# Attention of a two-layer diffusion step: eight of the gates' modulation blocks on VectorE from a ring of their own, two units a round on TensorE, output tiles in the last round

## The chip, the cores and the metric

The kernel runs on one core of a Trainium2 chip. The time is that of one execution on the device in microseconds; a kernel's time is the median of several executions. Beside it stands one execution taken with the hardware profiler, whose trace gives start and length of every instruction.

The names used below: TensorE (PE in the profile) multiplies matrices and turns 128x128 blocks, ScalarE (ACT) and VectorE (DVE) work element by element, GpSimd (POOL) does little here, SyncE (SP) issues nearly all transfers. PSUM is the memory of eight banks that TensorE writes; ScalarE and VectorE read it.

## The reference, cut to what matters

One step of a backbone with two layers, for 384 tokens (128 of a prompt, 256 of a sample, a grid 64 wide) and a model width of 1024, all in float32. Each layer is a mixer and a gated ConvFFN, each with an adaptive norm ahead of it and a gate on its residual. The change lies in the attention mixer of layer 0.

```python
mod = silu(cond) @ w_ada + b_ada            # (2, 6*1024): one row for the prompt, one for the sample
sm, cm, gm, sf, cf, gf = split(mod, 6)      # shift, scale, gate of the mixer; the same of the FFN
# layer 0, mixer
h = rmsnorm(x, g) * (1 + cm) + sm
q, k, v = qkv_proj(h, w_qkv)                # 16 heads of 64
# prompt tokens: softmax(q k^T / 8) v among themselves
# sample tokens: softmax over (window of the grid, with a bias per head, and 128 cached context keys)
x = x + gm * (attn(q, k, v) @ w_o)
# layer 0, FFN
h = rmsnorm(x, g2) * (1 + cf) + sf
x = x + gf * (silu(conv(h @ w_up_gate)) * conv(h @ w_up_value)) @ w_down
# layer 1 likewise, its mixer a gated MLP over chunks; then a last rmsnorm
# outputs: y of prompt and sample, and the keys and values of the prompt
```

## The kernel before, in words

**Layout and products.** Everything is kept with features on the 128 partitions and tokens along the row: `x[k]`, k = 0..7, is 128x384. A float32 product is made of three matmuls on halves: `split` (lines 116 to 118) rounds a tensor to `hi` on ScalarE and takes `lo` = source − `hi` on VectorE, and `mac` (lines 110 to 114) adds hi·hi, hi·lo and lo·hi. A tile of output (128x384 out of 8 row blocks) is thus 24 matmuls. A unit of weights (128x1024, 512 KB) comes through one of three staging buffers `st`, is split by `ready` into one of five `hi`/`lo` pairs, and is fetched three units ahead by SyncE's queue. The normalized input `h` is kept as `hhi`, `hlo` (8 blocks each).

**Modulations.** Layer 0's SM and CM are made ahead of the attention. The other pieces are made in one of two ways. `Ada` (lines 167 to 221) makes layer 0's GM, SF and CF on TensorE: a unit is one row block k of one piece, loaded (512 KB, tile `adw`) and multiplied in four small matmuls at four column positions (line 197), 24 units in all. After k = 7 ScalarE copies the sums out (`ada_sb`, line 202), and `flush`, called ahead of the next unit, turns them with two transposes (line 213) into a bank that VectorE adds the bias from (line 215; for CF also line 126). `AdaV` (lines 225 to 259) makes all the others, 56 blocks, on VectorE: two dot products of a 128x1024 block with the broadcast silu(c) (line 255, one for each of the two rows c) and an add (line 257). Those run in the FFNs and the gMLP. All blocks of both classes go through one ring of four buffers `adw`.

**Rounds.** The attention runs in eight rounds t = 0..7, one pair of heads each. The order of the instructions on TensorE, ScalarE, VectorE and SyncE is as the code is written (`tc.manual_schedule`, left at `written.__exit__`); behind that a scheduler orders them. One round, b = 0, 1 being the two blocks of 128 sample queries:

1. `scores(0)` (line 612: six pairs of matmuls, prompt queries included), then SyncE issues the next round's cached keys (`kT`) and bias rows (`btr`); `exps(0)`: on VectorE bias and maximum in one pass (line 619, into `st`), on ScalarE the exponentials with their sums (line 629).
2. `turn` of the last round's first head (lines 644, 646), `normalized` (a reciprocal, line 634, and products, line 636), ScalarE's copies of the turned blocks (`pT`, lines 651, 652).
3. `products` with the next pair's key weights (24 matmuls), `ready` for the next unit, `scores(1)`, and `keys(t+1)`: ScalarE copies two parts of the products beside the cached part in `kT` (lines 567, 568), then splits all 512 columns into `khi` and `klo`.
4. `exps(1)`, `turn` of the other head, `normalized`; `products` with the next query weights, `ready`, `bias` (line 602: the next round's bias in `bt`), `queries` (`qhi` line 577 on ScalarE, `qlo` line 578 on VectorE).
5. `values(t-1)` (line 661, split into `ohi`, `olo`), `ada.run(3)`, and the loads of three further units.

TensorE's queue, and each of the others, is worked off strictly in this order, so a wait on one engine holds what is written behind it.

**Last round.** It has no products. `ada.run(3)` stands between `scores(1)` and the turning. Then the output projection: tiles m = 0..3 start on the blocks k = 0..5, take blocks 6 and 7 as the last two rounds' values arrive; `flush` of CF; the four tiles' last blocks with `residual` (line 382: x += gate · bank, two instructions a tile, and ScalarE's squares for the next norm). Behind the written order come tiles 4 to 7 with their residuals, then the FFN (`norm_first`): on VectorE, GpSimd and ScalarE the root of the mean square (lines 317 to 321) and its spread `R` (line 359), then the last blocks of `h` (lines 334 to 338), while TensorE starts on the blocks that are ready. There `ada_v.start` loads silu's input and ScalarE makes silu(c) (line 246).

## Time and profile before

| | us |
|---|---|
| median of three runs | 1010.93 (1010.9 to 1011.51) |
| the profiled execution | 1011.21 |
| its span (first to last instruction) | 1009.4 |
| granted TensorE clock, mean | 0.997 |
| first round's first line 619 on VectorE | 68.83 |
| eighth round's | 176.10 |
| the FFN's first matmul behind the output tiles | 224.90 |

A span counts from the first instruction; the execution's time has 1.8 us more around it. All times of rows are from the span's start. A row of the timeline reads: start, length of the instruction or of the joined group, engine, line, operation, output<-input, sizes, count, and in brackets the idle time ahead of it and what ended it. A row of the windows gives for one stretch the busy time and count of TensorE, its weight loads, VectorE, ScalarE and GpSimd, then the granted clock as a share of full speed, the share of the DMA engines and GB/s. A row of the waits gives the total of a kind of wait, how often it came and the longest.

### The profile page before, as it was taken

To read this page: it belongs to the slowest core of one execution; us is meant where nothing else is said; L and a number is where in the kernel's file an instruction comes from. 1 tells how busy PE (TensorE), PEld (TensorE's weight loads), DVE (VectorE), ACT (ScalarE), POOL (GpSimd) and SP (SyncE) were. 2 spreads that over 40 slices of the span, in tenths; PEclk is the share of its full clock that TensorE was granted. 3 is DMA by queue.
4 is the path that set the end of the run, shared out by engine and by line. 5 is a ranking of instruction groups with operands and counts; after the bars stand their busy time and mean duration, and the time that the engine had idled before them with its cause. 6 is when DMAs were issued, how large, how long until landed. Compare 5 with 4: busy or idle time off the path is not lost.

```text
span 1009.4 us, 15920 instructions
## 1 busy us (share of the span) xinstructions
PE 991.1 (98%) x6007; PEld 940.8 (93%) x6008; DVE 778.3 (77%) x1597; ACT 479.8 (48%) x839; POOL 15.8 (2%) x31
## 2 busy tenths in 40 slices
PE   8999999999999999999999999999999999999996
PEld 6788888799999999999998889999999999999996
DVE  5656666488999888999889999687598777777652
ACT  4455655467655454433463334433385444443331
POOL 1000000000000000000000000000000000000000
PEclk9999999999999999999999999999999999999999
DMA  8766465634465554567728765466235434345521
GB/s 332 284 217 209 167 214 168 225 116 135 127 201 167 150 163 144 180 213 224 237 97 272 237 191 181 161 201 187 94 91 166 140 125 126 126 115 168 167 73 63
DMA packets 53020, 172.96 MB, mean 171 GB/s; under 512 B 6016, under 2 KB 11152, under 8 KB 52944
## 3 DMA queue, kind: packets, MB, share of 16 engines
q1 hardware_dynamic: 51840, 169.33, 51.8%
q0 software_dynamic: 528, 1.32, 0.3%
q10 hardware_dynamic: 576, 1.31, 0.3%
q8 instruction: 47, 0.77, 0.3%
q14 instruction: 29, 0.24, 0.1%
HBM read 169.31 MB, written 2.62 MB: 170 GB/s over the span
## 4 chain that ended last, share of the span: by engine, by line
PE 92%; DMA 3%; DVE 2%; ACT 1%; issue 1%; POOL 0%; POOLq 0%; SPq 0%; ACTq 0%
PE bank L113 28%; PE bank L114 28%; PE bank L112 28%; DMA kT<-in_ckT 1%; PE bank L883 1%; PE bank L661 1%; PE bank L644 1%; PE bank L612 1%; PE bank L150 1%; PE bank L197 1%; DMA adw<-in_w_ada 1%; DMA lo<-in_x 0%; PE bank L449 0%; POOL ry L319 0%; PE bank L291 0%
## 5 line engine op out<-in xcount | busy, mean ns | idle before, releaser
L105 ACT CAST hi<-st 128x1024 fp32r<-128x1024 f32 (+1 forms) x184 | 189.3, 1030 | 296.2 <-PE bank L113 237.6
L114 PE MATMUL bank<-hhi,lo 128*128 128x384 f32 (+1 forms) x960 | 325.0, 339 | 0.2 <-DVE lo L118 0.2
L113 PE MATMUL bank<-hlo,hi 128*128 128x384 f32 (+1 forms) x960 | 324.7, 338 | 0.0
L112 PE MATMUL bank<-hhi,hi 128*128 128x384 f32 (+1 forms) x960 | 324.6, 338 | 0.0
L106 DVE TENSOR_TENSOR lo<-st,hi 128x1024 fp32r<-128x1024 f32 (+1 forms) x184 | 220.1, 1198 | 64.6 <-ACT hi L105 64.5
L114 PEld LDWEIGHTS bank<-hhi,lo 128*128 128x128 f32 x960 | 181.1, 189 | 0.5 <-DVE lo L118 0.5
L112 PEld LDWEIGHTS bank<-hhi,hi 128*128 128x128 f32 x960 | 181.0, 189 | 0.4 <-ACT kT L568 0.2
L113 PEld LDWEIGHTS bank<-hlo,hi 128*128 128x128 f32 x960 | 180.4, 188 | 0.1
L255 DVE CUSTOM_DVE_ANT_0 junk<-adw,cs 128x1024 bf16<-128x1024 f32 x112 | 136.5, 1219 | 1.0
L113 PE MATMUL bank<-alo,hi 128*128 128x384 f32 x352 | 118.3, 336 | 0.0
L114 PE MATMUL bank<-ahi,lo 128*128 128x384 f32 x352 | 118.3, 336 | 0.0
L112 PE MATMUL bank<-ahi,hi 128*128 128x384 f32 x352 | 118.1, 336 | 0.0
L114 PEld LDWEIGHTS bank<-ahi,lo 128*128 128x128 f32 x352 | 66.2, 188 | 0.0
L113 PEld LDWEIGHTS bank<-alo,hi 128*128 128x128 f32 x352 | 66.2, 188 | 0.0
L112 PEld LDWEIGHTS bank<-ahi,hi 128*128 128x128 f32 x352 | 66.2, 188 | 0.0
L112 PE MATMUL bank<-hi,hhi 128*128 128x512 f32 x144 | 58.1, 403 | 0.4 <-ACT hhi L440 0.4
L113 PE MATMUL bank<-lo,hhi 128*128 128x512 f32 x144 | 56.9, 395 | 0.1
L114 PE MATMUL bank<-hi,hlo 128*128 128x512 f32 x144 | 56.7, 394 | 0.0
L382 DVE SCALAR_TENSOR_TENSOR x<-bank,mod,x 128x128 f32<-128x128 f32 x64 | 23.8, 412 | 34.6 <-PE bank L114 34.5
L113 PE MATMUL bank<-mlo,hi 128*128 128x384 f32 x128 | 43.6, 341 | 0.0
L112 PE MATMUL bank<-mhi,hi 128*128 128x384 f32 x128 | 43.3, 338 | 0.0
L114 PE MATMUL bank<-mhi,lo 128*128 128x384 f32 x128 | 43.3, 338 | 0.0
(174 smaller groups left out, 1279.6 us busy)
## 6 DMA issues: line engine op xcount, KB each, us to landing
st<-in_w_up SPq DMA_DIRECT2D x88, 512.0 KB, 3.6
adw<-in_w_adaT SPq DMA_DIRECT2D x56, 512.0 KB, 3.6
adw<-in_w_ada SPq DMA_DIRECT2D x40, 512.0 KB, 5.6
st<-in_w_down SPq DMA_DIRECT2D x32, 512.0 KB, 3.6
st<-in_w_qk SPq DMA_DIRECT2D x16, 512.0 KB, 3.5
st<-in_w_gu SPq DMA_DIRECT2D x16, 512.0 KB, 4.1
st<-in_w_gv SPq DMA_DIRECT2D x16, 512.0 KB, 4.3
st<-in_w_gout SPq DMA_DIRECT2D x16, 512.0 KB, 4.6
```

Of the source, the lines that this page charges most:

```text
L105: nc.scalar.copy(hi[:, :n], st[:, :n])
L106: nc.vector.tensor_tensor(lo[:, :n], st[:, :n], hi[:, :n].bitcast(F32), ALU.subtract)
L112: nc.tensor.matmul(out, a[0], b[0], start=start, stop=False)
L113: nc.tensor.matmul(out, a[0], b[1], start=False, stop=False)
L114: nc.tensor.matmul(out, a[1], b[0], start=False, stop=stop)
L150: nc.tensor.matmul(pa[32 * j:32 * j + 32, 0:P], cond_s[:, 4 * hf + kk, :], w[hf][:, kk, P * q:P * q + P], start=(kk == 0), stop=(kk == 3), ...
L197: nc.tensor.matmul(self.pa[32 * j:32 * j + 32, 0:256], cond_s[:, k, :], t[:, 256 * j:256 * j + 256], start=(k == 0), stop=(k == KD - 1), t ...
L255: tc.keep_in_program_order(nc.vector.tensor_tensor_reduce(self.junk, t, self.cs[c], 1.0, 0.0, ALU.mult, ALU.add, m[:, c:c + 1]))
L382: nc.vector.scalar_tensor_tensor(x[m][:, a:b], ps[:, a:b], mod(l, gate, m, c), x[m][:, a:b], ALU.mult, ALU.add)
L612: nc.tensor.matmul(sc[hh][:, cols], q[qp][HS[hh], qs:qs + P], k[kp][HS[hh], ks], start=i == 0, stop=i == 2)
L644: nc.tensor.transpose((ta[:, o:o + P] if g < 2 else tb[:, o - 512:o - 512 + P]), pr[:, b, g * P:g * P + P], ident)
L661: nc.tensor.matmul(pv[64 * hh:64 * hh + 64, cols], vv[:, P * t + 64 * hh:P * t + 64 * hh + 64], pT[hh][:, o:o + n], start=start, stop=stop ...
```

## The change

**Rings and shares.** The ring of four becomes two rings of two, `adw` and `adb`. `Ada` keeps SF and CF alone: 16 units, two ahead of the rounds, two in each of rounds 0 to 6, none in the last. GM of layer 0 goes to `AdaV` as eight blocks in ring `adb`. For these, silu(c) is made ahead of the first keys, and each round does one block on VectorE: one dot product (`half(0)`) behind `exps(0)`, the other with the add (`half(1)`) behind the second `normalized`. `AdaV`'s other 56 blocks stay where they were and use both rings in turn.

**Keys.** `keys` splits three parts (128 cached columns, and 256 and 128 columns straight from the products' bank) into `khi` and `klo` with no copy ahead; the prompt's keys for the output are copied by ScalarE afterwards (`sk`).

**Order within a round.** The next pair's cached keys and bias rows are issued one round earlier, ahead of the modulation loads on SyncE. `bias` moves up between `exps(1)` and `normalized`. `flush` has its own place between the second products and `values`.

**Last round.** It leaves the loop behind `exps(1)`; output tiles 0 and 1 stand between its steps, `flush` of CF comes between tile 1 and `values(6)`, tile 2 around `values(7)`. Tiles 3 to 7 are in the written order, each with the residual of the tile three before it; residuals 5 to 7 are behind it. `ohi` and `olo` of blocks 6 and 7 lie in `hhi` and `hlo`, which the products no longer need then.

```diff
-ADA_BUFS = 4
+ADA_BUFS = 2
...
-            order = [(0, GM), (0, SF), (0, CF)]
+            order = [(0, SF), (0, CF)]
...
         def one(self, l, pc, k, t):
-            self.flush()
...
+            self.todo = (one(0, GM) + both(1, SM, CM)[:8]
...
+        def half(self, c, l, pc, k, t):
+            m = mods[l][:, pc, k]
+            tc.keep_in_program_order(nc.vector.tensor_tensor_reduce(
+                self.junk, t, self.cs[c], 1.0, 0.0, ALU.mult, ALU.add, m[:, c:c + 1]))
+            if c:
                 nc.vector.tensor_scalar(m, m, b_ada[:, l, pc * 8 + k:pc * 8 + k + 1], None, ALU.add)
...
-        def keys(t, kT, p):
-            nc.scalar.copy(kT[:, 0:256], p[:, 0:256])
-            nc.scalar.copy(kT[:, 384:512], p[:, 256:384])
-            nc.gpsimd.dma_start(skT_out[:, t, :], kT[:, 0:NPR])
+        def keys(t, ck, p):
             k = [wkp.tile([P, 512], F32R, name=n, tag=n) for n in ("khi", "klo")]
-            split(*k, kT)
+            for o, src in ((256, ck), (0, p[:, 0:256]), (384, p[:, 256:384])):
+                s = slice(o, o + src.shape[1])
+                split(k[0][:, s], k[1][:, s], src)
+            sk = wkp.tile([P, NPR], F32, name="sk", tag="sk", bufs=1)
+            nc.scalar.copy(sk, p[:, 0:NPR])
+            nc.gpsimd.dma_start(skT_out[:, t, :], sk)
...
             e = exps(0, sc, pr, pc)
+            ada_v.half(0, *blocks[0])
...
+            bias(btr)
             normalized(*e)
-            if not last:
-                p = products()
-                ready()
-                bias(btr)
-                Q = queries(p)
-                if old is not None:
-                    values(t - 1, pT)
-                ada.run(3)
-                ada.load(3)
+            ada_v.half(1, *blocks.pop(0))
+            p = products()
+            ready()
+            Q = queries(p)
+            ada.flush()
+            if old is not None:
+                values(t - 1, pT)
+            if t < NPAIR - 2:
+                kT, btr = cache(t + 2), bias_load(t + 2)
+            ada.run(2)
+            ada.load(2)
+            if t < NPAIR - 2:
+                blocks.append(ada_v.load(1))
...
         output(0, range(6), ps_mm)
+        pT.append(turned(1, turn(*old[1])))
+        normalized(*e)
         ready()
-        values(6, pT, ps_sc)
+        pv = bank(ps_sc)
         output(1, range(6), ps_sc)
+        ada.flush()
+        values(6, pT, pv)
         ready()
+        ada_v.half(1, *blocks.pop(0))
...
-        output(2, range(7), ps_mm)
-        ready()
+        output(2, range(5), ps_mm)
         values(7, pT)
-        output(3, range(7), ps_sc)
-        ada.flush()
-        for m in range(4):
+        output(2, (5, 6))
+        for m in range(3):
             output(m, (7,))
-            residual(0, GM, m, out[m][1], (0, SF, CF))
-            if m == 1:
+        for m in range(3, KD):
+            output(m, range(KD), (ps_sc, ps_ta, ps_ad, ps_mm, ps_sc)[m - 3])
+            if m < KD - 1:
                 ready()
+            residual(0, GM, m - 3, out[m - 3][1], (0, SF, CF))
         written.__exit__(None, None, None)
-        for m in range(4, KD):
-            output(m, range(KD), ps_mm if m % 2 else ps_sc)
-            if m < KD - 2:
-                ready()
+        for m in range(KD - 3, KD):
             residual(0, GM, m, out[m][1], (0, SF, CF))
```

VectorE in a middle round, from the split of the keys to the split of the queries, as it stands before (line 619 with its `ISA` rows is the bias with the maximum, line 634 the reciprocal, line 602 the bias for the next round):

```order
159 L118 TENSOR_TENSOR klo<-kT,khi 128x512
160 L619 ISA bank,st<-bank,bt 128x384
161 L619 ISA st 128x1
162 L619 ISA bank,st<-bank,bt 128x384
163 L619 ISA st 128x1
164 L634 RECIPROCAL st<-st 128x2
165 L636 TENSOR_SCALAR pr<-pr,st 128x384 x2
166 L118 TENSOR_TENSOR lo<-st,hi 128x1024
167 L602 TENSOR_TENSOR bt<-mask,btr 128x3x128 x2
168 L578 SCALAR_TENSOR_TENSOR qlo<-bank,qhi 128x384
```

The same place behind the change, where line 636 is the bias with the maximum, line 619 the next round's bias, line 260 the dot product of `half` and line 263 its add:

```order
184 L118 TENSOR_TENSOR klo<-ck,khi 128x128
185 L118 TENSOR_TENSOR klo<-bank,khi 128x256
186 L118 TENSOR_TENSOR klo<-bank,khi 128x128
187 L636 ISA bank,st<-bank,bt 128x384
188 L636 ISA st 128x1
189 L636 ISA bank,st<-bank,bt 128x384
190 L636 ISA st 128x1
191 L619 TENSOR_TENSOR bt<-mask,btr 128x3x128 x2
192 L651 RECIPROCAL st<-st 128x2
193 L653 TENSOR_SCALAR pr<-pr,st 128x384 x2
194 L260 ISA junk,mod_129<-adb,cs_628 128x1024
195 L260 ISA mod_129 128x1
```

The subtraction of the keys is in three parts, the bias stands ahead of the reciprocal, and the dot product stands between the normalized rows and the weights' `lo`, which with `qlo` follows as before.

TensorE at the end of a round in which a piece of `Ada` has been completed, before (`pT`, `V` are `values`, `adw` with `cond_s` the units, `ident` with `ada_sb` the flush, `khi` with `qhi` the next scores):

```order
441 L661 MATMUL bank<-pT,V 64x256 x2
442 L661 MATMUL bank<-pT,V 64x128 x2
443 L197 MATMUL bank<-adw,cond_s 32x256 x8
444 L213 MATMUL bank<-ident,ada_sb 128x128 x2
445 L197 MATMUL bank<-adw,cond_s 32x256 x4
446 L612 MATMUL bank<-khi,qhi 128x384 x2
```

And behind the change:

```order
562 L215 MATMUL bank<-ident,ada_sb 128x128 x2
563 L678 MATMUL bank<-pT,V 64x256 x2
564 L678 MATMUL bank<-pT,cv 64x256 x2
565 L678 MATMUL bank<-pT,V 64x256 x2
566 L678 MATMUL bank<-pT,V 64x128 x2
567 L199 MATMUL bank<-adw,cond_s 32x256 x8
568 L629 MATMUL bank<-khi,qhi 128x384 x2
```

The two transposes no longer stand between two units of the same round; they stand ahead of `values`, a round behind the last unit of their piece.

VectorE where the residuals start, before (`olo` rows are `values` of pairs 6 and 7, lines 215 and 126 the bias and gain of CF, line 382 the residual):

```order
248 L118 TENSOR_TENSOR olo_169<-bank,ohi_161 128x384
249 L118 TENSOR_TENSOR lo<-st,hi 128x1024 x2
250 L118 TENSOR_TENSOR olo_170<-bank,ohi_162 128x384
251 L215 TENSOR_TENSOR mod_129<-bank,b_ada 128x16
252 L126 SCALAR_TENSOR_TENSOR mod_129<-mod_129,prm 128x16
253 L382 SCALAR_TENSOR_TENSOR x_99<-bank,mod_129,x_99 128x128
```

And behind the change (`hlo` from `bank` is now the values' rest):

```order
301 L217 TENSOR_TENSOR mod_129<-bank,b_ada 128x16
302 L126 SCALAR_TENSOR_TENSOR mod_129<-mod_129,prm 128x16
303 L118 TENSOR_TENSOR hlo<-bank,hhi 128x384
304 L118 TENSOR_TENSOR lo<-st,hi 128x1024
305 L260 ISA junk,mod_129<-adb,cs_628 128x1024
306 L260 ISA mod_129 128x1
307 L263 TENSOR_SCALAR mod_129<-mod_129,b_ada 128x2
308 L118 TENSOR_TENSOR hlo<-bank,hhi 128x384
309 L118 TENSOR_TENSOR lo<-st,hi 128x1024
310 L394 SCALAR_TENSOR_TENSOR x_99<-bank,mod_129,x_99 128x128
```

CF's bias and gain stand ahead of both values' subtractions and no longer between the last values and the first residual.

More of the change, by code (lines that the diff above doesn't have):

```diff
@@ L129, in gain, with ada_tile @@
             ALU.add, ALU.mult)
+    def ada_tile(ring):
+        tag = ("adw", "adb")[ring % 2]
+        return adp.tile([P, D], F32, name=tag, tag=tag)
     def ada_load(f, late=False):
@@ L134, in ada_load @@
         for hf in range(2):
-            st = adp.tile([P, D], F32, name="adw", tag="adw")
+            st = ada_tile(hf)
             if late:
@@ L181, in load @@
                 l, pc, k = self.todo.pop(0)
-                t = adp.tile([P, D], F32, name="adw", tag="adw")
+                t = ada_tile(0)
                 nc.sync.dma_start(t, w_ada[k * P:(k + 1) * P, (pc - GM) * D:(pc - GM + 1) * D])
@@ L259, in run @@
                     gain(l, pc, slice(k, k + 1))
+        def run(self, n):
+            for _ in range(n):
+                block = self.load(len(self.todo))
+                for c in range(2):
+                    self.half(c, *block)
     ada_v = AdaV()
@@ L407, in attention @@
         cv = pool.tile([P, D], F32, name="cv")
-        ohi = [pool.tile([P, NT], F32R, name=f"ohi{t}") for t in range(NPAIR)]
-        olo = [pool.tile([P, NT], F32R, name=f"olo{t}") for t in range(NPAIR)]
+        ohi = [pool.tile([P, NT], F32R, name=f"ohi{t}") for t in range(6)] + [hhi[:, t, :NT] for t in (6, 7)]
+        olo = [pool.tile([P, NT], F32R, name=f"olo{t}") for t in range(6)] + [hlo[:, t, :NT] for t in (6, 7)]
         acc = [bank(q) for q in (ps_mm, ps_mm, ps_mm, ps_sc, ps_sc, ps_ta)]
@@ L509, in attention @@
             sb = ada_products(aw.pop(k + 1))
+            if k == 5:
+                ada_v.start(csp)
             if k + 3 < KD:
@@ L653, in turned, with values @@
             return pT
-        def values(t, pT, pool=ps_mm):
-            pv = bank(pool)
+        def values(t, pT, pv=None):
+            pv = bank(ps_mm) if pv is None else pv
             def part(hh, cols, vv, o, n, start, stop):
@@ L676, in attention @@
         nc.sync.dma_start(cv, cv_in)
-        ada.load(3)
+        ada.load(2)
+        blocks = [ada_v.load(1) for _ in range(2)]
         ready()
@@ L683, in attention @@
         v_out(1)
+        ada_v.silu()
+        ada_v.junk = tmp.tile([P, D], BF16, name="junk", tag="R0")
         nc.gpsimd.dma_start(sv_out, V[:, 0, :])
@@ L690, in attention @@
         Q = queries(p)
+        kT, btr = cache(1), bias_load(1)
+        ada.run(2)
+        ada.load(2)
         old = None
@@ L908, in gmlp @@
             residual(1, GM, m, ps, (1, SF, CF))
+    csp = ctx.enter_context(tc.tile_pool(name="cs", bufs=1))
     with tc.tile_pool(name="att", bufs=1) as pool, tc.tile_pool(name="attw", bufs=2) as wkp:
         attention(pool, wkp)
[L913 to L914 removed]
+    ada_v.junk = csp.tile([P, D], BF16, name="junk")
     with tc.tile_pool(name="ffn0", bufs=1) as pool, tc.tile_pool(name="ffn0w", bufs=2) as wkp:
```

45 lines of the change are left out of this document (18 added, 27 removed).

## The prediction

> **What bounds the kernel now.** I read the page first, then the waits of TensorE between 60 and 226 us, then the timeline of VectorE and TensorE there. The page:
>
> ```profile
> span 1009.4 us, 15920 instructions
> PE 991.1 (98%) x6007; PEld 940.8 (93%) x6008; DVE 778.3 (77%) x1597; ACT 479.8 (48%) x839; POOL 15.8 (2%) x31
> ```
>
> TensorE is busy 98% of the span, so a gain must come out of work taken from it or out of its few waits. These are, in the attention:
>
> ```profile
> PE bank L197 <- DMA adw<-in_w_ada: 2.0, 3, 0.7
> PE bank L112 <- DVE x L382: 1.9, 1, 1.9
> PE bank L213 <- ACT ada_sb L202: 1.0, 2, 0.5
> PE bank L612 <- ACT qhi L577: 0.6, 1, 0.6
> PE bank L612 <- DVE qlo L578: 0.6, 2, 0.3
> ```
>
> Each round's first line 619 on VectorE follows the round's first scores at once, so I use it as the round's mark S. Marks of rounds 0, 1, 3 and 7:
>
> ```profile
> 68.83 0.57 DVE L619 CUSTOM_DVE_ANT_0 bank<-bank,bt 128x384 f32<-128x384 f32 x1 [0.82 <-PE bank L612]
> 81.44 0.57 DVE L619 CUSTOM_DVE_ANT_0 bank<-bank,bt 128x384 f32<-128x384 f32 x1 [0.81 <-PE bank L612]
> 113.52 0.57 DVE L619 CUSTOM_DVE_ANT_0 bank<-bank,bt 128x384 f32<-128x384 f32 x1 [0.79 <-PE bank L612]
> 176.10 0.57 DVE L619 CUSTOM_DVE_ANT_0 bank<-bank,bt 128x384 f32<-128x384 f32 x1 [0.77 <-PE bank L612]
> ```
>
> Round 0 takes 12.61 us, the six rounds 1 to 6 together 94.66. TensorE's own time for a full round shows where it hardly waits, from one round's first scores to the next ones:
>
> ```profile
> 109.91 1.07 PE L197 MATMUL bank<-adw,cond_s 128*32 128x256 f32 x16
> 112.41 0.44 PE L612 MATMUL bank<-khi,qhi 64*128 64x384 f32 x2
> 126.04 1.50 PE L197 MATMUL bank<-adw,cond_s 128*32 128x256 f32 x24
> 127.47 0.45 PE L612 MATMUL bank<-khi,qhi 64*128 64x384 f32 x2
> 128.22 0.44 PE L612 MATMUL bank<-khi,qlo 64*128 64x384 f32 x2
> ```
>
> 127.47 − 112.41 = 15.06 us, and three units of Ada take 127.47 − 126.04 = 1.43, one 0.48. At 109.91 the three units with a flush among them take 2.50, so a flush costs 1.07, half of it the wait for `ada_sb`.
>
> **The sum, part by part.** It is made against the profiled execution, 1011.21 us, which lies 0.28 above the median 1010.93.
>
> *Prologue.* Two units are new there, +0.95. They stand where TensorE waits 0.6 for `qhi`, and fill that: +0.35. If the wait stays behind them, +0.95.
>
> *Rounds 1 to 6.* A unit less leaves 15.06 − 0.48 = 14.58 of TensorE's work. One flush remains (SF; GM's is gone) without its wait: 0.57 at most, 0.4 taken with the first small waits. 6 × 14.58 + 0.4 = 87.9, against 94.66: −6.8. This holds only if VectorE, which gets more, keeps ahead. Its rows of round 3, then the first round's, then three of the same dot product in the FFN:
>
> ```profile
> 116.80 0.18 DVE L634 RECIPROCAL st<-st 128x4 f32<-128x4 f32 x1 [1.80 <-ACT pc L629]
> 118.61 1.23 DVE L118 TENSOR_TENSOR lo<-st,hi 128x1024 fp32r<-128x1024 f32 x1 [0.45 <-ACT hi L117]
> 121.20 0.69 DVE L118 TENSOR_TENSOR klo<-kT,khi 128x512 fp32r<-128x512 f32 x1 [1.37 <-ACT khi L117]
> ...
> 74.53 0.69 DVE L118 TENSOR_TENSOR klo<-kT,khi 128x512 fp32r<-128x512 f32 x1
> 75.14 0.56 DVE L619 CUSTOM_DVE_ANT_0 bank<-bank,bt 128x384 f32<-128x384 f32 x1
> 77.06 0.17 DVE L634 RECIPROCAL st<-st 128x2 f32<-128x2 f32 x1 [0.79 <-ACT pr L629]
> 78.00 1.23 DVE L118 TENSOR_TENSOR lo<-st,hi 128x1024 fp32r<-128x1024 f32 x1
> 79.14 1.02 DVE L602 TENSOR_TENSOR bt<-mask,btr 128x384 f32<-128x384 f32 x2
> 80.08 0.55 DVE L578 SCALAR_TENSOR_TENSOR qlo<-bank,qhi 128x384 fp32r<-128x384 f32 x1
> ...
> 285.39 1.22 DVE L255 CUSTOM_DVE_ANT_0 junk<-adw,cs 128x1024 bf16<-128x1024 f32 x1
> 286.80 0.22 DVE L257 TENSOR_SCALAR mod<-mod,b_ada 128x2 f32<-128x2 f32 x1
> ```
>
> `half(0)` (1.22) lies in the 1.80 that VectorE waits for the exponentials: nothing; without that cover it costs VectorE its length. The chain from there: `lo` starts at S + 5.09 (118.61) and takes 1.14 (78.00 to 79.14). Then come the keys. Today `klo` waits 1.37 for ScalarE, which waits for the cached columns:
>
> ```profile
> ACT khi L117 <- DMA kT<-in_ckT: 8.3, 6, 1.8
> ```
>
> With the load a round earlier and no copy, that wait goes. In its place `klo` is in three parts; the whole takes 0.61 (74.53 to 75.14), and by columns and a fixed part I estimate 0.21, 0.35 and 0.21. The last two read the same bank as ScalarE's casts, and in the new order the third cast waits for the second subtraction: 0.4 for that turn, so 1.15 in all. **0.4 is not in the trace**; with the casts ahead it is 0, and with both casts of about 0.4 in turn it is 0.8. Then the steps as the rows have them, start to start: line 619 twice 1.13 (77.06 less the 0.79 wait and 75.14), `bias` 0.94 in place of that wait, the normalized rows 0.94, `half(1)` with its add 1.55 (285.39 to 286.80, and most of the add's 0.22), `lo` 1.14. So `qlo` starts at S + 5.09 + 1.14 + 1.15 + 1.13 + 0.94 + 0.94 + 1.55 + 1.14 = 13.1 and ends at 13.65. TensorE, whose scores come 1.11 ahead of the mark (112.41 to 113.52), starts them at S + 13.47 and reaches the pair that needs `qlo` about 0.5 later (128.22 − 127.47 with a wait of 0.3 in it), at 13.97. **Spare: 0.3 us.** It is thin, but TensorE sets the round, and I take −6.8; between no turn and twice the turn the spare is 0.7 to −0.1.
>
> The row above shows `khi` and `klo` today taken from `kT`, in no bank at all. [...]
>
> *Round 0.* There are no transposes and no values for TensorE to do, so the same chain sets the round. By its rows the `lo` ends at 74.53, S + 5.7; the keys to 6.85; 1.13 + 0.94 + 0.94 + 1.55 + 1.14 to `qlo` at 12.55; from `qlo` to the next mark 81.44 − 80.08 = 1.36: 13.9, against 12.61: +1.3. It is the price of the dot product where nothing covers it. Ends: 0.5 (no turn, `bias` all in the gap) to 2.
>
> *Last round.* Rows of TensorE from mark 7 on, then the windows behind its longest wait:
>
> ```profile
> 177.37 0.35 PE L612 MATMUL bank<-khi,qlo 64*128 64x384 f32 x2
> 181.01 0.64 PE L197 MATMUL bank<-adw,cond_s 128*32 128x256 f32 x8 [0.64 <-DMA adw<-in_w_ada]
> 206.62 0.41 PE L112 MATMUL bank<-ohi,hi 128*128 128x384 f32 x1 [1.88 <-DVE x L382]
> 212.42 0.34 PE L112 MATMUL bank<-ohi,hi 128*128 128x384 f32 x1
> 224.90 0.34 PE L112 MATMUL bank<-hhi,hi 128*128 128x386 f32 x1
> ...
> 206.00:208.00 2.00, 1.38 (x6) 1.41 (x7) 1.41 (x6) 1.50 (x5) 0.00 (x0) 0.84 0.00 0
> 208.00:210.00 2.00, 2.00 (x8) 2.00 (x8) 1.57 (x3) 2.00 (x3) 0.00 (x0) 0.50 0.00 0
> 210.00:212.00 2.00, 2.00 (x11) 2.00 (x10) 2.00 (x5) 1.95 (x5) 0.00 (x0) 0.80 0.38 90
> ```
>
> The three units with their waits on loads take from 177.72 to 181.65, −3.9, all gone. At 206.62 TensorE waits for a bank that a residual frees; CF's flush and the last values stood ahead of that residual on VectorE. Written out, the next tile uses another bank: −1.9. Behind the wait the clock falls to 0.50: 96 matmuls take 224.90 − 206.62 = 18.28, at the pace of the last 72 (12.48 / 72 = 0.173) 16.64: −1.6. Added: tile 1's weights have their `lo` behind the normalized rows on VectorE, the flush and the turn must wait for copies on ScalarE: each up to one step like the `lo` above (1.14), less what TensorE still has queued; I take +0.9 of 0 to 2. Sum −6.5.
>
> [...] The row shows 1.88, then 0.50; the measurement decides. [...]
>
> *Start of the FFN.* Three residuals now lie behind the last tile, and blocks 6 and 7 of `h` share memory with the values, so their first halves wait for the last tile. The chain today:
>
> ```profile
> 228.40 0.72 PE L291 MATMUL bank<-ones,sqacc 128*128 128x2 f32 x6
> 232.42 0.83 PE L310 MATMUL bank<-ident,rr 128*128 128x128 f32 x6
> 245.33 0.47 DVE L338 SCALAR_TENSOR_TENSOR hlo<-t,mod,hhi 128x256 fp32r<-128x256 f32 x1
> ```
>
> The first two rows are the sums of squares and the spread on TensorE, the third the last `hlo`, which ends at 245.80. TensorE does four tiles on blocks without the norm first, then 21 matmuls of a fifth before the eighth normalized block is wanted: 117 × 0.173 = 20.3 from 224.90, with some 1.3 for the sums and the spread 246.5, and `hlo` comes second: 0.8 spare. I put the chain 1.6 later (an estimate: two residuals more, about the time of a row like `hlo`'s 0.47 for each of their instructions): +0.8, of 0 to 4. Silu's work on ScalarE has gone from there, which speaks for the lower end.
>
> Sum: 0.35 − 6.8 + 1.3 − 6.5 + 0.8 = −10.85. 1011.21 − 10.85 = 1000.36, less 0.28: **1000.1 us**.
>
> **The rivals.**
>
> - *VectorE's chain sets the rounds* (0.2). The spare of 0.3 rests on estimates of the keys and of starts. Overrun by 0.5 to 0.8 in seven rounds: +3.5 to +5.6, 1003.6 to 1005.7. For it: VectorE gets a block more a round, 1.22 + 1.55. Against: the keys' wait of 1.37 goes.
> - *The saving comes back at the FFN's start* (0.08): the chain of the norm 3 to 5 us later, 0.8 spare, so 1.4 to 3.4 above my term: 1001.5 to 1003.5.
> - *The change doesn't take the last round's stall away* (0.03): VectorE is still late at the first residual, −1.9 and −1.6 don't come: 1003.6. For it: VectorE gets a dot product in that stretch. Against: the flush leaves it and three tiles lie between.
> - *The half clock stays though the wait goes* (0.02): it would have another cause than the 1.88, and the 1.6 don't come: 1001.7. Against: the rows show it right behind that wait. [...]
> - *Slower: bias rows late in every round* (0.05). `bias` now stands ahead of the normalized rows, the dot product, `lo` and `qlo` in VectorE's queue. Its load:
>
> ```profile
> btr<-in_rpb SPq DMA_DIRECT2D x16, 109.5 KB, 6.8
> ```
>
> It is issued behind two weight loads, whose buffer the last `lo` frees (S' − 1.5, by the chain above), and wanted at S' + 8.5: 10 us for 6.8. A landing at 10 + 0.3 + 10.85/7 = 11.9 us in each of seven rounds eats the gain; from 12.2 on the kernel is slower by more than 2 us (1013), at 13 it is 7 × 1.1 = 7.7 slower (1018.6). Against it: five 512 KB loads a round share the queue, as many as before.
>
> **How the numbers follow.** The forecast with its own ends (round 0 at 0.5 to 2, stalls 0 to 2, FFN 0 to 2.5) has 0.62: 997.5 to 1003. The range reaches down to 996.5 (no turn, no new stall, no FFN stall, a little shorter rounds) and up over the first rival to 1005.5; beyond lie part of that rival and the slower one. Measurements tell 0.2%, 2.0 us, from no change. Faster: 0.93, all but the slower rival and a little of the overrun; within it 0.02; slower 0.05.
>
> **What would show it.** Right: marks 14.6 apart in rounds 1 to 6 and 13.9 in round 0, no wait of TensorE on `qlo` above 0.3, no granted clock under 0.9 between 195 and 215, no row of TensorE waiting for `adw` or a residual, and the FFN's start near 213. Wrong: waits on `qlo` in each round (first rival), on `btr` by VectorE (the last), a long wait of TensorE on `h` 22 us behind the FFN's start (second), the granted clock at 0.50 before it (third). A time above 1005.5 means that VectorE holds the rounds.

## The result, and the profile after

| | before | changed |
|---|---|---|
| median, us | 1010.91 (1009.16 to 1011.51, 4 runs) | 1000.80 (1000.13 to 1001.20, 4 runs) |
| profiled execution, us | 1011.21 | 1000.85 |
| its span, us | 1009.4 | 998.0 |
| granted clock, mean | 0.997 | 0.999 |

The ratio is 0.9893 with a 95% interval of 0.9876 to 0.9911: 10.1 us faster, at 1000.80, where 1000.1 had been forecast. The page of the changed kernel:

```profile
span 998.0 us, 15825 instructions
PE 982.9 (98%) x5942; PEld 934.9 (94%) x5942; DVE 797.4 (80%) x1652; ACT 476.3 (48%) x846; POOL 15.8 (2%) x31
```

TensorE lost 8.2 us of busy time, VectorE got 19.1. TensorE's waits between 60 and 230 us, changed kernel:

```profile
PE bank L629 <- DVE qlo L595: 1.3, 1, 1.3
PE bank L322 <- DVE rr L336: 0.6, 1, 0.6
PE bank L114 <- DVE lo L118: 0.5, 2, 0.3
```

The waits for `adw` (2.0), for the residual (1.9), for `ada_sb` (1.0) and for `qhi` (0.6) are gone. `qlo` had two waits of 0.3 each; it now has one of 1.3, in round 0. None of the waits left stands in rounds 1 to 6, and the one for `rr` stands behind the FFN's start. The marks of rounds 0, 1 and 7 on VectorE (line 636 is the old line 619), TensorE's first matmul of the FFN and a window of the clock where the stall had been:

```profile
68.33 0.57 DVE L636 CUSTOM_DVE_ANT_0 bank<-bank,bt 128x384 f32<-128x384 f32 x1 [0.85 <-PE bank L629]
81.87 0.57 DVE L636 CUSTOM_DVE_ANT_0 bank<-bank,bt 128x384 f32<-128x384 f32 x1 [0.82 <-PE bank L629]
169.90 0.57 DVE L636 CUSTOM_DVE_ANT_0 bank<-bank,bt 128x384 f32<-128x384 f32 x1 [0.91 <-PE bank L629]
212.19 0.34 PE L112 MATMUL bank<-hhi,hi 128*128 128x386 f32 x1
...
201.00:203.00 2.00, 2.00 (x14) 2.00 (x13) 1.56 (x5) 2.00 (x4) 0.00 (x0) 1.00 0.66 238
```

The differences of these places from those of before, beside the prediction's terms:

| stage | before, us | changed, us | difference | predicted |
|---|---|---|---|---|
| to mark 0 | 68.83 | 68.33 | −0.50 | +0.35 |
| round 0 | 12.61 | 13.54 | +0.93 | +1.3 |
| rounds 1 to 6 | 94.66 | 88.03 | −6.63 | −6.8 |
| mark 7 to the FFN's start | 48.80 | 42.29 | −6.51 | −6.5 |
| from there to the end of the span | 784.5 | 785.8 | +1.3 | +0.8 |
| span | 1009.4 | 998.0 | −11.4 | −10.85 |

The executions differ by 10.1 (medians) to 10.4 us (profiled), the spans by 11.4. The rest lies around the span: 1.8 us in the profile of before and 2.9 in that of the changed kernel. In the 51 executions of before that ran beside the experiments this part was 1.8 to 1.9 each time; in the nine of the changed kernel it was 1.9 to 3.3. So the change lengthens it in some executions, by up to 1.4 us. The prediction had no term for that, and what causes it was not settled.

### The profile page after: what moved, and what is told of

Its sections match the earlier page's. It is cut to its first block, busy times and chain, and to the rows that moved or that the text cites. A ratio compares the mean times of both kernels' runs of the same rounds, so it can differ in the third digit from the quotient of the medians.

```text
span 998.0 us, 15825 instructions
## 1 busy us (share of the span) xinstructions
PE 982.9 (98%) x5942; PEld 934.9 (94%) x5942; DVE 797.4 (80%) x1652; ACT 476.3 (48%) x846; POOL 15.8 (2%) x31
## 4 chain that ended last, share of the span: by engine, by line
PE 94%; DVE 2%; ACT 1%; issue 1%; POOL 1%; DMA 1%; POOLq 0%; SPq 0%; ACTq 0%
PE bank L113 29%; PE bank L114 29%; PE bank L112 29%; PE bank L678 1%; PE bank L629 1%; PE bank L912 1%; PE bank L661 1%; PE bank L155 1%; PE bank L199 1%; POOL ry L331 1%; DMA lo<-in_x 1%; PE bank L322 0%; DVE lo L118 0%; PE bank L303 0%; DVE bank L636 0%
## 5 line engine op out<-in xcount | busy, mean ns | idle before, releaser
L113 PE MATMUL bank<-hlo,hi 128*128 128x384 f32 (+1 forms) x976 | 330.5, 339 | 0.1
L112 PE MATMUL bank<-hhi,hi 128*128 128x384 f32 (+1 forms) x976 | 330.1, 338 | 0.0
L114 PE MATMUL bank<-hhi,lo 128*128 128x384 f32 (+1 forms) x976 | 329.9, 338 | 0.2 <-DVE lo L118 0.2
L114 PEld LDWEIGHTS bank<-hhi,lo 128*128 128x128 f32 x976 | 184.1, 189 | 0.7 <-DVE lo L118 0.5
L112 PEld LDWEIGHTS bank<-hhi,hi 128*128 128x128 f32 x976 | 184.0, 189 | 0.8 <-ACT hi L105 0.4
L113 PEld LDWEIGHTS bank<-hlo,hi 128*128 128x128 f32 x976 | 183.4, 188 | 0.6 <-DVE hlo L118 0.3
L260 DVE CUSTOM_DVE_ANT_0 junk<-adb,cs 128x1024 bf16<-128x1024 f32 x72 | 87.8, 1219 | 0.5
L260 DVE CUSTOM_DVE_ANT_0 junk<-adw,cs 128x1024 bf16<-128x1024 f32 x56 | 68.3, 1220 | 0.5
L112 PE MATMUL bank<-hi,hhi 128*128 128x512 f32 x144 | 58.1, 404 | 0.4 <-ACT hhi L453 0.4
```

The lines of the kernel that those rows point to most:

```text
L112: nc.tensor.matmul(out, a[0], b[0], start=start, stop=False)
L113: nc.tensor.matmul(out, a[0], b[1], start=False, stop=False)
L114: nc.tensor.matmul(out, a[1], b[0], start=False, stop=stop)
L260: tc.keep_in_program_order(nc.vector.tensor_tensor_reduce(self.junk, t, self.cs[c], 1.0, 0.0, ALU.mult, ALU.add, m[:, c:c + 1]))
```

## The experiments

Each kernel ran beside the kernel before on the same chip; there the latter's median was 1011.9 to 1012.7, and its times lay between 1008.8 and 1015.1. The changed kernel once more gave 1000.37 (999.62 to 1000.91, ratio 0.9880, 0.9862 to 0.9899).

> The changed kernel once more, with no edit, beside the three below: 1000.8, and in its profile the same rounds of 14.6 us.

Its marks 0, 1 and 7 were 68.33, 81.86 and 169.88, its FFN's start 212.17. Between this profile and the first one of the changed kernel the stages differ by 0.03 us at most, so the profiles below are compared by stage. Only the stage up to mark 0 differs from profile to profile, for a reason given under the prologue below. The differences in time below are between medians, against 1000.80 where the kernel did not run beside the repeated one.

| kernel | median, us | mark 0 | mark 1 | mark 7 | FFN's start | span |
|---|---|---|---|---|---|---|
| changed | 1000.80 and 1000.37 | 68.33 | 81.87 | 169.90 | 212.19 | 998.0 |
| GM on TensorE | 1003.31 | 70.03 | 82.46 | 174.69 | 217.01 | 1002.5 |
| late loads | 1009.18 | 68.56 | 82.28 | 179.37 | 221.72 | 1007.1 |
| third dot product | 1006.83 | 68.26 | 83.20 | 175.97 | 218.25 | 1003.9 |
| old end | 1005.55 | 68.08 | 81.62 | 169.63 | 215.84 | 1002.2 |
| old residuals | 1001.99 | 68.71 | 82.24 | 170.25 | 214.63 | 999.9 |
| before, units early | 1011.75 | 69.63 | 82.87 | 177.18 | 225.72 | 1010.2 |
| before, units early, tile ahead | 1011.22 | 68.72 | 81.99 | 175.93 | 222.27 | 1007.1 |
| block ahead | 999.78 | 72.11 | 84.63 | 172.64 | 214.93 | 1000.9 |
| block first | 998.72 | 68.43 | 80.65 | 168.67 | 210.97 | 996.7 |
| two tiles behind | 1001.64 | 68.44 | 81.97 | 170.00 | 212.31 | 999.0 |
| block first, two tiles behind | 1000.01 | 68.42 | 80.63 | 168.66 | 210.95 | 997.6 |

**What the move to VectorE is worth.** GM's units back on TensorE, no dot products in the attention:

```diff
-            order = [(0, SF), (0, CF)]
+            order = [(0, GM), (0, SF), (0, CF)]
...
-            ada_v.half(0, *blocks[0])
...
-            ada.run(2)
-            ada.load(2)
+            ada.run(3)
+            ada.load(3)
```

> The changed kernel with GM's eight units back on TensorE (three units a round and three ahead of the rounds) and no dot products on VectorE in the attention. First theory: 0.48 us more in each of rounds 1 to 6 and ahead of the rounds, 0.3 for a flush, and 0.9 less in round 0: 2.7 us slower, 1003.5. So the move to VectorE is worth only about a quarter of the gain. Rival: the rounds are set by VectorE, then taking its dot products away gives back what TensorE's units cost: 1000 to 1001.

1003.31 (ratio 0.9919, 0.9906 to 0.9931), 2.5 us slower than the changed kernel; the spans are further apart, 1001.2 to 1002.5 against 997.8 to 998.0, since the part around the span is 1.8 to 1.9 here. Round 0 took 12.43 (1.1 less), rounds 1 to 6 together 92.23 (4.2 more): the units' 2.9, and 1.0 of waits for `ada_sb`, since a piece here ends between two units of one round and the next unit needs its bank; the rest are GM's flush and what turns on it. By the medians the move is worth a quarter of the gain, by the spans about a third. The rival falls, since rounds 1 to 6 grew.

**What the early loads are worth.** Cached keys and bias rows go back behind the first scores:

```diff
             scores(0, Q, K, sc)
+            if not last:
+                kT, btr = cache(t + 1), bias_load(t + 1)
             e = exps(0, sc, pr, pc)
...
-            if t < NPAIR - 2:
-                kT, btr = cache(t + 2), bias_load(t + 2)
             ada.run(2)
```

> The changed kernel with the cached keys and the bias rows loaded where they were before, behind the same round's first scores. First theory: the keys wait for the load again, line 636's second pass starts some 0.9 us later in a round (8.3 instead of 7.4 behind the mark); of that TensorE's spare of 0.7 us hides most in rounds 1 to 6 (0.1 to 0.4 each), round 0 pays it whole: 1.5 to 3 us slower, about 1003. Rival one: there is no spare, 0.9 us in each of seven rounds, 1007. Rival two: the loads' place does nothing, 1000.8.

1009.18 (ratio 0.9978, 0.9968 to 0.9989): 8.4 us slower, more than any of the three said. Rounds 1 to 6 took 16.6, 17.25, 17.3, 15.8, 15.1 and 15.0. Rows of ScalarE, then of TensorE, in round 2 (mark 98.88):

```profile
107.88 0.30 ACT L117 CAST khi<-ck 128x128 fp32r<-128x128 f32 x1 [3.94 <-DMA ck<-in_ckT]
...
111.86 0.43 PE L678 MATMUL bank<-pT,V 128*64 128x256 f32 x1 [1.47 <-ACT pT L668]
```

ScalarE waits 3.94 for the cached columns, 9.0 behind the mark (the same cast ran 4.9 behind it in the changed kernel). Its later work, the copies of the turned blocks, comes late with it, and TensorE waits for them, 4.5 us in rounds 1 to 3; on `qlo` it waits 0.2 in each of four rounds. So the first theory had the load right, but not the size nor the place: line 636's second pass stands 10.6 behind the mark here, where it had said 8.3. On SyncE the load is issued 0.7 us behind the mark, at 99.61; before the change the same load left 0.9 ahead of its mark, at 112.66. Ahead of it in SyncE's queue stand four loads of 512 KB in both kernels, one of them now VectorE's block. Keys and bias rows moved together in this run; VectorE waits for no bias row in it, so the cached keys are what it shows.

**How much room VectorE has.** One dot product more in rounds 0 to 6:

```diff
+            ada_v.half(0, *blocks[0])
             ada_v.half(1, *blocks.pop(0))
             p = products()
```

> The changed kernel with one dot product more on VectorE in each of rounds 0 to 6 (the first half computed a second time). First theory: 1.14 us against a spare of 0.73 in front of TensorE's need of qlo: 0.4 us in each of rounds 1 to 6 and 1.14 in round 0, 3.5 us slower, 1004.3. Rival one: no spare, 1.14 in each, 8 us slower, 1008.8. Rival two: VectorE has room, only round 0 pays, 1 us slower, 1002.

1006.83 (ratio 0.9954, 0.9941 to 0.9967): 6 us slower. Round 0 grew by 1.4, round 1 from 14.65 to 16.05, rounds 2 to 6 from 14.63 (14.85 in round 3, with the flush) to 15.34. TensorE's waits, the longest of them, and the clock behind it:

```profile
PE bank L629 <- DVE qlo L595: 4.5, 6, 2.5
82.30 0.44 PE L629 MATMUL bank<-khi,qlo 64*128 64x384 f32 x2 [2.54 <-DVE qlo L595]
...
83.00:85.00 2.00, 2.00 (x11) 1.91 (x10) 1.80 (x7) 0.48 (x2) 0.00 (x0) 0.50 0.67 261
```

Round 1 pays for the half clock behind round 0's wait and does not wait on `qlo` itself. From round 2 on a dot product, 1.26 from its start to the next one's, costs 0.7 a round, so the room is 0.5 to 0.6. That lies between the first theory (0.73) and rival one (none), nearer the first; the prediction had 0.3.

**The last round's order.** First the whole of the old order, put into the changed kernel:

```diff
-        output(0, range(6), ps_mm)
         pT.append(turned(1, turn(*old[1])))
         normalized(*e)
+        output(0, range(6), ps_mm)
         ready()
...
         output(3, range(7), ps_sc)
+        ada.flush()
+        for m in range(4):
+            output(m, (7,))
+            residual(0, GM, m, out[m][1], (0, SF, CF))
```

Here the residual of tile 6 overwrites a block of values that tile 7 still reads, so its last tile is wrong. It is used for its times alone.

> The rounds as changed, the last round's order as before (output tiles 0 and 1 behind the turning, flush of CF behind tile 3, residuals 0 to 3 straight behind their tiles). First theory: the stall of 1.9 us at the first residual and the half clock behind it (1.6 us) come from this order, so they are back: about 3.5 us slower than the changed kernel, 1004.3, with a granted clock near 0.5 for about 2 us. A wait at the turning of up to 1.5 us may come on top, since no units cover it now. Rival: the last round gained only by the three units that left it; then no stall and no half clock, and at most 1.5 us slower, 1000.8 to 1002.3.

1005.55, 4.8 slower. Rows of TensorE, each with the windows behind it:

```profile
173.42 0.88 PE L661 MATMUL bank<-ident,pr 128*128 128x128 f32 x6 [2.17 <-ACT pT L668]
200.03 0.41 PE L112 MATMUL bank<-ohi,hi 128*128 128x384 f32 x1 [1.84 <-DVE x L394]
...
174.00:176.00 2.00, 2.00 (x11) 2.00 (x10) 1.55 (x4) 0.69 (x1) 0.00 (x0) 0.62 0.17 70
176.00:178.00 2.00, 2.00 (x8) 2.00 (x7) 1.18 (x6) 1.48 (x5) 0.00 (x0) 0.53 0.49 121
200.00:202.00 2.00, 1.97 (x11) 2.00 (x12) 1.29 (x4) 2.00 (x5) 0.00 (x0) 1.00 0.00 0
```

Both waits that the theory named are there; the one at the turning, put at up to 1.5, is 2.17. The clock fell behind the first and stayed at 1.00 behind the second. Then the flush and the residuals alone, with tile 0 ahead of the turning:

```diff
         output(1, range(6), ps_sc)
-        ada.flush()
         values(6, pT, pv)
...
+        output(3, range(7), ps_sc)
+        ada.flush()
+        for m in range(4):
+            output(m, (7,))
+            residual(0, GM, m, out[m][1], (0, SF, CF))
```

> The changed kernel with the residuals' and the flush's old place alone (tile 0 still ahead of the turning; the flush of CF behind tile 3, residuals straight behind their tiles, tiles 4 to 7 in the scheduler's order). First theory: the stall of 1.8 to 1.9 us at the first residual is back; the clock falls behind it in some executions and not in others, so 1.9 to 3.5 us slower than the changed kernel, 1002.7 to 1004.3, and the FFN's norm comes sooner, up to 0.6 back. Rival: with the units gone VectorE is in time for the residual, no stall, 1000.2 to 1001.

1001.99 (ratio 0.9906, 0.9893 to 0.9920), 1.2 slower by the medians, which their intervals do not tell apart, and less than the 1.9 to 3.5 expected. The spans do not overlap: 999.0 to 999.9 against 997.8 to 998.0. By stage, 2.1 more from mark 7 to the FFN's start (44.38), with the row:

```profile
197.76 0.41 PE L112 MATMUL bank<-ohi,hi 128*128 128x384 f32 x1 [1.84 <-DVE x L394]
```

So the stall comes with the old place of the flush and the residuals, and not with the units. It is worth 1.8 us; the 1.6 of half clock did not come with it.

**What the last round's units were worth.** The kernel before, its units one round earlier:

```diff
         Q = queries(p)
+        ada.run(3)
+        ada.load(3)
         old = None
...
-            if last:
-                ada.run(3)
-            else:
+            if not last:
                 K = keys(t + 1, kT, p)
```

> The kernel before with one edit: the units of Ada run one round earlier, three ahead of the rounds and none in the last. First theory: the last round loses the units and their waits on loads (3.9 us), the part ahead of the rounds gains 0.85, the residual's stall and the half clock stay: 3.0 us faster than before, 1007.9. Rival one: the stall comes from the late units, so it goes with them: 6.5 us faster, 1004.4. Rival two: the units only covered a wait for the turned blocks' copies, which now shows: 1.5 us faster or less, 1009.4 to 1010.9.

1011.75, ratio 1.0001 (0.9988 to 1.0014): nothing. From mark 7 to the FFN's start 48.54 against 48.80. The 3.9 us of units and waits on loads went. In their place came a wait of 2.18 and a second stretch of half clock behind it, some 1.7 us more:

```profile
180.96 1.54 PE L644 MATMUL bank<-ident,pr 128*128 128x128 f32 x6 [2.18 <-ACT pT L651]
207.43 0.41 PE L112 MATMUL bank<-ohi,hi 128*128 128x384 f32 x1 [1.88 <-DVE x L382]
...
180.00:182.00 2.00, 1.04 (x5) 1.04 (x6) 1.32 (x5) 2.00 (x6) 0.00 (x0) 0.66 0.87 342
182.00:184.00 2.00, 2.00 (x9) 2.00 (x8) 1.73 (x4) 0.24 (x1) 0.00 (x0) 0.50 0.03 12
208.00:210.00 2.00, 2.00 (x8) 2.00 (x7) 1.57 (x5) 2.00 (x4) 0.00 (x0) 0.50 0.00 0
```

The turning needs the bank that ScalarE has still to copy out (line 651), and the units had covered that. Rival two has the mechanism, though even its 1.5 us did not come. The same with the first six blocks of tile 0 in their place:

```diff
+            if last:
+                output(0, range(6), ps_mm)
             if old is not None:
                 pT.append(turned(1, turn(*old[1])))
```

> The kernel before with two edits: Ada's units a round earlier, and the first six blocks of output tile 0 ahead of the last turning. First theory: the units had covered TensorE's wait of 2.2 us for the bank that the turned blocks lie in; with a tile in their place that wait and the half clock behind it go, so about 3 us faster than before, 1008 by the table's median. Rival: the wait at the turning is only moved to the next step, 1 us faster or less.

1011.22, ratio 0.9998 (0.9986 to 1.0011): nothing again by the medians. The profiled execution is the shortest of the twelve, 1008.99, since no half clock came in it. The turning no longer waits, but the next step on TensorE does:

```profile
184.57 0.43 PE L661 MATMUL bank<-pT,V 128*64 128x256 f32 x1 [2.38 <-ACT pT L651]
...
206.00:208.00 2.00, 2.00 (x13) 2.00 (x12) 1.56 (x5) 2.00 (x5) 0.00 (x0) 1.00 0.00 0
```

`values(6)` needs the copies of both heads, and the second comes behind the round's last exponentials. The wait has only moved. In the changed kernel tile 1 and the flush stand between the turning and `values(6)` (TensorE reaches it at 179.47, behind copies that end at 178.9), and it waits for neither. In this profile the clock stayed at 1.00 behind the wait for the residual, 1.88 as before; in the profile of before it fell to 0.50.

**What is left in the changed kernel.** Round 0 pays for its dot products. They go ahead of the rounds:

```diff
+        ada_v.half(0, *blocks[0])
         p = products()
         K = keys(0, kT, p)
+        ada_v.half(1, *blocks.pop(0))
...
-            ada_v.half(0, *blocks[0])
+            if t:
+                ada_v.half(0, *blocks[0])
```

> The changed kernel with the first block's two dot products ahead of the rounds (around the first keys), where VectorE is idle, and none in round 0. First theory: VectorE sets round 0 alone; without the 1.4 us there, the round takes TensorE's 12.1 instead of 13.5: 1.4 us faster, 999.4, with the first mark at most 0.2 later. Rival: the first keys or queries come later by the same amount, no gain.

999.78 (999.23 to 1002.82, ratio 0.9891, 0.9875 to 0.9907), not to be told from the changed kernel. In the profiled execution, which was the longest of the four (span 1000.9, the others 997.3 to 997.5), round 0 took 12.52, but mark 0 came 3.8 later. VectorE's first of the two, and TensorE's clock behind it:

```profile
64.46 1.23 DVE L260 CUSTOM_DVE_ANT_0 junk<-adb,cs 128x1024 bf16<-128x1024 f32 x1 [4.69 <-DMA adb<-in_w_adaT]
...
72.00:74.00 2.00, 2.00 (x8) 2.00 (x7) 1.48 (x6) 0.57 (x3) 0.00 (x0) 0.50 0.78 168
```

The block had not landed in this execution. So, with the same edit, it is also loaded ahead of the third weight unit, and the cached values last:

```diff
-        for _ in range(3):
+        for _ in range(2):
             fetch()
+        blocks = [ada_v.load(1)]
+        fetch()
         kT, btr = cache(0), bias_load(0)
-        nc.sync.dma_start(cv, cv_in)
         ada.load(2)
-        blocks = [ada_v.load(1) for _ in range(2)]
+        blocks.append(ada_v.load(1))
+        nc.sync.dma_start(cv, cv_in)
```

> The changed kernel with the first block's dot products ahead of the rounds, and that block loaded ahead of the third weight unit and the other small loads (cached values last). First theory: the wait of 4.7 us for the block is gone, the first mark comes as in the changed kernel (within 0.3), round 0 takes 12.1: 1.4 us faster, 999.4. Rival: the queue is full there (390 GB/s), what is put ahead only makes the next load late, and TensorE waits for that: no gain.

998.72 (998.63 to 998.86; ratio 0.9864, 0.9846 to 0.9882): 1.65 us below the changed kernel's 1000.37 beside it, and each of its four times is below each of the changed kernel's five. VectorE's first dot product and mark 1:

```profile
59.57 1.23 DVE L260 CUSTOM_DVE_ANT_0 junk<-adb,cs 128x1024 bf16<-128x1024 f32 x1 [0.27 <-ACT cs L250]
...
80.65 0.56 DVE L636 CUSTOM_DVE_ANT_0 bank<-bank,bt 128x384 f32<-128x384 f32 x1 [0.82 <-PE bank L629]
```

Round 0 is 12.2, and mark 0 is within 0.1 of the changed kernel's. This beats both kernels, and the rival falls. The other place that waits, the sums behind the last residual, with residuals two tiles behind instead of three:

```diff
-            residual(0, GM, m - 3, out[m - 3][1], (0, SF, CF))
+            for r in ((0, 1) if m == 3 else (m - 2,)):
+                residual(0, GM, r, out[r][1], (0, SF, CF))
```

> The changed kernel with each residual two tiles behind its output tile where it is three. First theory: one residual less lies behind the last tile, so the sums come about 1 us sooner and TensorE's wait of 0.6 for the root of the mean square goes: 0.6 to 1.2 us faster, 999.6 to 1000.2. Rival: the residuals now wait for their tile on VectorE and hold the weights' second halves behind them; TensorE waits for those, 0 to 2 us slower.

1001.64 (1000.91 to 1003.39), 1.3 slower than the changed kernel beside it. The FFN's wait for `rr` is gone, and in its place, 25 us behind the FFN's start, TensorE has this one for a weight's second half:

```profile
237.58 0.44 PE L114 MATMUL bank<-hhi,lo 128*128 128x384 f32 x1 [1.75 <-DVE lo L106]
```

This is the rival's wait, though later than it said. On VectorE this `lo` (line 106, at 236.31) now stands behind four rows of the FFN's first gate; in the changed kernel it stands ahead of them. That order is the scheduler's, not the written one. With both edits:

> Both edits, the first block ahead of the rounds and residuals two tiles behind: the gains add, 2.0 to 2.6 us faster than the changed kernel, 998.2 to 998.8. If either rival above holds, its part is missing.

1000.01 (999.57 to 1000.16), 1.3 above the first edit alone: the second costs there what it costs by itself.

## Why the prediction was right

The forecast was 0.7 us from the measured time, and part of that closeness is luck. In the profiled executions the span shrank by 0.55 more than the sum says, and the part around it grew by 1.0, for which the sum had no term. Inside the span, the prologue and round 0 came out better than their terms and the FFN's start worse.

**Prologue, +0.35.** From the first key products to the first scores TensorE took 9.16 us before (58.32 to 67.48) and 9.51 behind (57.71 to 67.22): +0.35. The stage as a whole came out at −0.5. Of this, 0.2 is the wait for `qlo` at the first scores, which the units now cover. The other 0.6 is that the products themselves started sooner, which is not the change's doing. The trace's record of the clock has its first rise at 9.40 us before and at 5.75 in the changed kernel; ahead of it the same six transposes take 1.51, behind it 0.88:

```profile
5.81 1.51 PE L449 MATMUL bank<-ident,lo 128*128 128x128 f32 x6 [0.72 <-DMA lo<-in_x]
5.68 0.88 PE L462 MATMUL bank<-ident,lo 128*128 128x128 f32 x6 [0.59 <-DMA lo<-in_x]
```

Over all fourteen profiles, the ten with the first rise at 4.2 to 7.2 have the first key products at 57.5 to 58.1, the four with 9.3 to 10.8 (before, units early, GM on TensorE, block ahead) at 58.3 to 59.0. Both kinds occur among the variants of either kernel.

**Rounds 1 to 6, −6.8; measured −6.63.** TensorE sets them at 14.63 (14.85 with the flush): it is busy in all of the 88.03. The chain on VectorE came out as worked up to line 636, from mark 111.15 of the changed kernel:

```profile
116.23 1.23 DVE L118 TENSOR_TENSOR lo<-st,hi 128x1024 fp32r<-128x1024 f32 x1 [0.45 <-ACT hi L117]
118.32 0.29 DVE L118 TENSOR_TENSOR klo<-bank,khi 128x128 fp32r<-128x128 f32 x1 [0.33 <-ACT khi L117]
118.53 0.56 DVE L636 CUSTOM_DVE_ANT_0 bank<-bank,bt 128x384 f32<-128x384 f32 x1
123.85 0.55 DVE L595 SCALAR_TENSOR_TENSOR qlo<-bank,qhi 128x384 fp32r<-128x384 f32 x1
```

`lo` starts 5.08 behind the mark, the second pass of line 636 at 7.38 as worked, `qlo` at 12.70 (worked: 13.1). The 0.4 lies in three steps that were taken too long: the two passes of line 636 take 0.99 (taken: 1.13), the normalized rows 0.86 (0.94), `half(1)` with its add 1.40 (1.55). The turn between ScalarE and VectorE on one bank shows as 0.33, where 0.4 was taken for want of a row. In the trace the two engines take turns on different columns of one bank: ScalarE's last cast starts at 118.03, behind a wait of 1.36 for `klo`, where VectorE's middle subtraction ends (118.00). What the chip does without the turn no run here shows. The room, 0.3 in the sum, is 0.5 to 0.6 by the third dot product.

**Round 0, +1.3; measured +0.93.** VectorE sets it, shown by TensorE's wait of 1.3 on `qlo` and by the round's 12.2 where the dot products go ahead of it. The prediction's sign "no wait of TensorE on `qlo` above 0.3" left out this wait, which its own term for round 0 asks for. The term was 0.4 too large by the same three steps: the rows from line 636 to `qlo` take 5.32 (75.18 to 80.50), where 5.7 had been added up.

**Last round, −6.5; measured −6.51.** The sum is met to 0.01, which is luck, since its steps are not met as closely. "The three units with their waits on loads take from 177.72 to 181.65, −3.9, all gone" treats them as free to go. By the two kernels made from before, taking them out alone brings nothing: TensorE then waits 2.2 to 2.4 for ScalarE's copies of the turned blocks. By the traces, what makes the 3.9 real is that tiles 0 and 1 now stand ahead of the turning and of `values(6)`; the sum had those only as added stalls of 0.9. These stalls show as one wait of 0.27, for a `lo`; TensorE is idle 0.35 us in the whole stage (busy 41.94 of 42.29). Where the other 0.6 went was not settled. Tile 1's place alone was not tried. The stall at the first residual was put down rightly to what stood ahead of it on VectorE (old residuals: back at 1.84).

**Half clock, −1.6.** It did go with the wait in the profiled executions, against the rival that has it stay (1001.7): no window of the changed kernel between 195 and 217 is below 1.00. But the same wait of 1.84 to 1.88 with no fall of the clock, in three other profiles, shows that the term is no fixed price of the wait. Of the five profiles with that wait at the first residual, two have the half clock behind it (before and units early). By that count the term is worth about 0.6 on average (an estimate: two fifths of the 1.6). What decides was not shown. The spread of before fits: of its 51 executions beside the experiments, the 13 with a mean granted clock of 0.998 or more have spans of 1008.8 on average, the 20 with 0.995 or less 1011.2. Which stall each of them owes that to is not known.

**The FFN's start, +0.8; measured +1.3.** A size and a place that were off. The eighth block of `h` was in time; TensorE waited earlier, at the spread, for the root:

```profile
218.48 0.72 PE L303 MATMUL bank<-ones,sqacc 128*128 128x2 f32 x6
222.03 0.91 PE L322 MATMUL bank<-ident,rr 128*128 128x128 f32 x6 [0.61 <-DVE rr L336]
```

Between sums and spread lie 3.6 us here and 4.0 before, and the sums come 6.3 behind the FFN's start instead of 3.5. About 1.2 of the 1.3 is lost by the first tile on normalized blocks (19.4 behind the start instead of 18.2); of that 0.6 is this wait, and where the rest went is not settled.

**Bias rows late, the slower rival.** Its mechanism shows in no run: VectorE waits for no bias row, in the changed kernel or with late loads. Its neighbour does: with late loads the cached keys hold ScalarE, and the rounds grow to as much as 17.3. That the change puts these loads first is worth 8.4 us, a term that the sum used ("that wait goes") but gave no price of its own.

## What to carry to other kernels

Before counting an idle-looking stretch on the critical engine as a gain, ask what else would have waited there: the next two steps' inputs may arrive no sooner (here waits of 2.18 and 2.38 us came in place of the 3.9), and by these traces only other work placed ahead of both turned the stretch into time. Work in an engine's gaps cost nothing here as long as the chain to the next thing that the critical engine needs had room (0.5 to 0.6 us a round); measure that room by adding work until the time moves. Small loads that are wanted early belong ahead of large ones in a queue that also waits for buffers (8.4 us here). And before a stretch of half clock in one profile is counted as a gain, look in other profiles for the same wait without it (three of five here).

## What the runs showed of the hardware

The table has twelve waits of TensorE of 1.7 to 2.5 us from these profiles. Behind six of them the granted clock was 0.50, behind the other six 1.00:

| kernel | wait of TensorE, its end | granted clock behind |
|---|---|---|
| third dot product | 2.54, 82.30 | 0.50 |
| units early | 2.18, 180.96 | 0.50 |
| old end | 2.17, 173.42 | 0.50 |
| before | 1.88, 206.62 | 0.50 |
| units early | 1.88, 207.43 | 0.50 |
| block ahead | 1.68, 70.85, and one of 0.7 | 0.50 |
| tile ahead | 2.38, 184.57 | 1.00 |
| late loads | 2.24, 129.32 | 1.00 |
| tile ahead | 1.88, 205.56 | 1.00 |
| old end | 1.84, 200.03 | 1.00 |
| old residuals | 1.84, 197.76 | 1.00 |
| two tiles behind | 1.75, 237.58 | 1.00 |

By the trace's record of the clock these six stretches at 0.50 lasted 3.41 us each: 207.37 to 210.79 (before), 174.48 to 177.89 (old end), 82.74 to 86.15 (third dot product), 180.62 to 184.03 and 207.93 to 211.34 (units early), 70.77 to 74.18 (block ahead). In the profile of before, matmuls of 384 columns start 0.17 us apart ahead of the stretch and 0.32 apart in it.

The length of the wait does not tell the two kinds apart: 1.88 stands in both, and 2.38 and 2.24 left the clock at 1.00 where 1.68 with one of 0.7 did not. What decides was not shown.
